# Two modulation units ahead of the tokens, and the opening's four up blocks taken in turns on six PSUM banks

## The chip, the cores and the metric

The kernel runs on one core of a Trainium2 chip as one program. The time is device microseconds from the first to the last instruction of a run. The five engines have a queue each: TensorE (PE; its weight loads are listed apart as PEld), VectorE (DVE), ScalarE (ACT), GpSimd (POOL) and SyncE (SP), which issues most of the DMA transfers.

## The reference

One layer of a diffusion backbone on 256 context tokens and 256 latent tokens of width 2048: a half-step SwiGLU feed-forward, a mixer (attention and mLSTM heads), a second feed-forward and a norm. The change lies in the first feed-forward's up product:

```python
def adaln(x, g, mod, i):
    return rms_norm(x, g) * (1 + mod[:, i + 1, None, :]) + mod[:, i, None, :]

def half_step_ffn(x, mod, i, g, w_up, w_down):
    h = adaln(x, g, mod, i)
    a, b = jnp.split(h @ w_up, 2, axis=-1)
    return x + 0.5 * mod[:, i + 2, None, :] * ((jax.nn.silu(a) * b) @ w_down)

# mod = (silu(c) @ w_mod + b_mod), one for the latent and one for the context tokens
```

Everything is fp32. The kernel gets that on TensorE by splitting each operand into a rounded part hi and a rest lo, and by three matmuls: hi x hi, lo x hi, hi x lo.

## The kernel before, in words

The hidden width 5632 is cut into 44 blocks of 128 (index f), each with a gate half a and a value half b. Before the first four blocks (f = 0 to 3) can be multiplied, shift and scale have to be made from the condition vector and `w_m0`, and the tokens have to be normalised. The kernel does all this at once in an **opening** that walks the 16 tiles of K (128 features each) in nine blocks: (0,1), (1,2), then seven of two tiles.

For each block of K:

- `mod_unit` loads pieces of the modulation weights (tile `mraw`, 1 MiB, four buffers), one unit each for the scale and the shift of a single K tile, four for a block of two. `mod_sums` multiplies a unit with the condition vector `cP` on TensorE; ScalarE copies the sums to `row`, TensorE turns them (`mod_turned`), and VectorE reduces them into the shift SH and the scale SC. One unit in four is multiplied on VectorE with `cB`, the condition vector spread over the partitions (`spread`, by matmuls with ones).
- `to_hT` (for the first two blocks `x_scaled`) transposes the normalised tokens `xs`, and `affine_split` makes hhi (ScalarE) and h and hlo (VectorE): the scaled and shifted tokens, split.
- `products` multiplies the block's rows of the up weights of f = 0, 1, 2 with them, into six PSUM banks `pre`. One transfer brings the block's weights (tile `raw`, three buffers); `split` makes hi (ScalarE, L118) and lo (VectorE, in the opening shown under L78). The products of a block are woven between the modulation sums of the next one.

Ahead of the blocks, the four token tiles (two of context, two of latent tokens, 1 MiB each) are loaded, squared on ScalarE (`sumsq`, L153), and scaled on VectorE (`x_tile`); their first columns are transposed (`x_turned`).

VectorE and TensorE are wrapped by `Pinned` in the opening: their instructions run in the order in which the code issues them, and the profile shows them all under L78, the wrapper's line. The SP queue is pinned as well. ScalarE's order is left to a scheduler, which works it out when the kernel is built.

After the opening `tail(f, pre[f])` takes silu(a) x b of f = 0, 1, 2 and stores it to `hidd[0]` (tile `ca`); f = 3 is done alone with 96 matmuls on whole weight tiles (`load_split`); then `quad(1)` begins, the first of the strip products that do four blocks f by seven products of half the size. It reads weight tiles `chain` and `raw`, whose splits VectorE makes, and sums of tokens (`token_forms`: n1, s2, s4, s3; tile `sraw`, and the lo parts n1l, s2l, s4l), which VectorE makes as well. A quad has 14 steps of 24 matmuls, each behind the split of one weight tile in two halves.

Of the kernel before, what the change touches and what calls it, by code (L numbers as in the profile page):

```python
# [19 lines left out]
P = 128  # L20
# [13 lines left out]
PACE2 = 70 / 73  # L34

BLOCKS = ((0, 1), (1, 2)) + tuple((k, k + 2) for k in range(2, 16, 2))
FB = 4
CB = 512
NCB = D // CB
# [10 lines left out]
def tile_layer(ctx: ExitStack, tc: tile.TileContext, I: dict, out: bass.AP):  # L50
# [13 lines left out]
    def bank():  # L64
        return ps["mm"].tile([P, 512], F32, tag="mm", name="mm")
# [265 lines left out]
    def pin(ins):  # L331
        tc.keep_in_program_order(ins)
# [111 lines left out]
    hlo = hpool.tile([P, KT, 512], F32R, tag="hl", name="hlo")  # L444

    pre = [[bank(), bank()] for _ in range(NPRE)]
    with pool(name="st", bufs=1) as st:
        scratch.append(st)
        cP = st.tile([P, KT, 32], F32, name="cP")
        nc.gpsimd.memset(cP, 0.0)  # L450
        pc = tbank()
# [52 lines left out]
        for s in (CTX, LAT):  # L504
            for t in range(2):
                x = xs0[s, t] = st.tile([P, D], F32, name=f"xs{s}{t}")
                tc.keep_in_program_order(nc.sync.dma_start(x, xsrc[s][t * P : (t + 1) * P, :]))
        tc.keep_in_program_order(nc.sync.dma_start(vecs, I["vecs"]))
        diagonals = [diagonal(s) for s in (CTX, LAT)]
        spread(CTX, diagonals[0])  # L510
        x_tile(CTX, 0)
        x_turned(0, CTX, 0)
        spread(LAT, diagonals[1])
        for s, t in ((CTX, 1), (LAT, 0), (LAT, 1)):
            x_tile(s, t, s == LAT and t == 1)
            x_turned(0, s, t)
# [5 lines left out]
        prods = iter(())  # L522
        unit = iter(range(32))

        def mod_unit():
            raw = st.tile([P, 2048], F32, tag="mraw", name="mraw", bufs=4)
            tc.keep_in_program_order(nc.sync.dma_start(raw, I["w_m0"][next(unit)]))
            return raw
# [33 lines left out]
                biased(i, k0, k1)  # L562
            turns.clear()

        turns = []
# [76 lines left out]
    with pool(name="f1u", bufs=1) as f1u:  # L642
# [7 lines left out]
        def ca_tile():  # L650
            return f1u.tile([P, CB], F32, tag="ca", name="ca", bufs=2)

        def tail(f, pab):
            sa = ca_tile()
            nc.scalar.activation(sa, pab[0], AF.Silu)
            nc.vector.tensor_tensor(sa, sa, pab[1], op=ALU.mult)
# [7 lines left out]

        for c in range(2):
            first_chain(1, c)
        for f in range(NPRE):
            tail(f, pre[f])
        for f in range(NPRE, FB):
            pab = []  # L670
            for ab in range(2):
                wt = load_split(I["w_up1"][f, ab])
                b = bank()
                for k in range(KT):
                    mm3(b, *wt(slice(k * P, (k + 1) * P)), hhi[:, k, :], hlo[:, k, :], k == 0, k == KT - 1)
                pab.append(b)
            tail(f, pab)


        n1, s2, s4 = form("n", "n1"), form("s", "s2"), form("t", "s4")  # L680
# [66 lines left out]
        def c12_tile():  # L747
            return f1u.tile([P, CB], F32, tag="c12", name="c12", bufs=2)

        def quad(n, after=lambda step: None):  # L750

# [1458 lines left out]
```

## Time and profile before

| | |
|---|---|
| time, median of 3 runs | 2666.89 us (2665.67 to 2669.02) |
| span of the profiled execution | 2666.8 us |
| TensorE busy | 2609.9 us (98%) |
| VectorE busy | 2130.1 us (80%) |
| ScalarE busy | 1347.2 us (51%) |
| granted TensorE clock, mean | 0.996 |
| DMA, mean | 255 GB/s |

In the rows of the timeline the first number is the start in us from the start of the span, the second the duration, then engine, line, operation, output tile <- input tiles, shape. Brackets give the idle time just before it and what released it. "SPq" is a DMA issue on SP's queue; in the list of DMA issues the last number is the median time in us from issue to landing. x4 means four such instructions joined in one row.

### The profile page before, as it was taken

Reading aid. Unit: us, or ns where it says so; the run is one execution under the profiler, and the core shown is the slowest. Engines: PE = TensorE matmul, PEld = TensorE weight load, DVE = VectorE, ACT = ScalarE, POOL = GpSimd, SP = SyncE. Lnnn points to the kernel's source line nnn. Section 1 sums busy time; section 2 is a strip of 40 time slices with the busy share of each in tenths; the row PEclk is TensorE's granted clock in tenths of the full one; section 3 lists DMA queues with packets and bytes.
Section 4 is the critical chain, followed back from the end, with each engine's and each line's share of the span. In section 5 each row is a group of like instructions: output and inputs, shape, how many; then the busy total and the mean of one; then the engine's idle time right before and its main releaser. Section 6 shows DMA issues by size and latency. Waiting matters only on the chain. (4 is left out here: it accounts for less than half of the span.)

```text
span 2666.8 us, 33730 instructions
## 1 busy us (share of the span) xinstructions
PE 2609.9 (98%) x12718; PEld 2158.4 (81%) x12718; DVE 2130.1 (80%) x2901; ACT 1347.2 (51%) x1682; POOL 221.6 (8%) x271
## 2 busy tenths in 40 slices
PE   8999999999999999999999999999999999999998
PEld 4688887888888878888889888877888888888886
DVE  5797878878888788888886979797688777777867
ACT  4354444544444565444454346355476655555554
POOL 0000001100000100000110000121000000000001
PEclk9999999999999999999999999999999999999999
DMA  9979999999999989889986866574579998989975
GB/s 346 351 213 270 263 279 260 258 276 281 264 280 273 266 230 239 229 209 234 225 233 224 309 229 225 205 260 166 172 249 284 295 286 292 289 277 281 277 230 168
DMA packets 135027, 679.97 MB, mean 255 GB/s; under 512 B 14152, under 2 KB 23624, under 8 KB 73552
## 3 DMA queue, kind: packets, MB, share of 16 engines
q1 hardware_dynamic: 107504, 500.59, 50.9%
q0 software_dynamic: 27360, 177.22, 34.0%
q8 instruction: 100, 1.64, 0.2%
q14 instruction: 63, 0.52, 0.1%
HBM read 659.87 MB, written 17.89 MB: 254 GB/s over the span
## 5 line engine op out<-in xcount | busy, mean ns | idle before, releaser
L118 ACT ACTIVATE hi<-raw 128x1024 fp32r<-128x1024 f32 (+3 forms) x542 | 560.7, 1038 | 639.0 <-PE mm L142 473.0
L119 DVE TENSOR_TENSOR lo<-raw,hi 128x1024 fp32r<-128x1024 f32 (+1 forms) x524 | 630.0, 1209 | 277.2 <-ACT hi L118 260.0
L118 ACT ACTIVATE hi<-chain 128x1024 fp32r<-128x1024 f32 x320 | 337.5, 1059 | 259.1 <-PE mm L142 129.1
L119 DVE TENSOR_TENSOR lo<-chain,hi 128x1024 fp32r<-128x1024 f32 x320 | 387.4, 1222 | 97.6 <-ACT hi L118 95.0
L140 PE MATMUL mm<-hi,hhi 128*128 128x512 f32 (+3 forms) x1024 | 392.5, 385 | 6.5 <-DVE c L744 6.0
L141 PE MATMUL mm<-lo,hhi 128*128 128x512 f32 (+3 forms) x1024 | 388.0, 379 | 1.7 <-DVE lo L119 1.5
L142 PE MATMUL mm<-hi,hlo 128*128 128x512 f32 (+3 forms) x1024 | 387.5, 379 | 0.0
L198 DVE SCALAR_TENSOR_TENSOR junk<-sraw,cBh 128x1024 fp8e5<-128x1024 f32 x192 | 234.4, 1221 | 23.2 <-DMA sraw<-in_w_mt 20.9
L140 PEld LDWEIGHTS mm<-hi,hhi 128*128 128x128 f32 x1024 | 192.8, 189 | 39.5 <-ACT hi L118 4.5
L141 PEld LDWEIGHTS mm<-lo,hhi 128*128 128x128 f32 x1024 | 193.1, 189 | 33.9 <-DVE lo L119 2.8
L142 PEld LDWEIGHTS mm<-hi,hlo 128*128 128x128 f32 x1024 | 192.8, 188 | 33.8
L142 PE MATMUL mm<-hi,hid2l 128*128 128x512 f32 x352 | 137.3, 390 | 0.0
L140 PE MATMUL mm<-hi,hid2h 128*128 128x512 f32 x352 | 137.2, 390 | 0.0
L141 PE MATMUL mm<-lo,hid2h 128*128 128x512 f32 x352 | 137.1, 390 | 0.0
L140 PE MATMUL mm<-hi,h2hi 128*128 128x512 f32 x320 | 125.0, 391 | 1.5 <-DVE sab L1802 1.5
L141 PE MATMUL mm<-lo,h2hi 128*128 128x512 f32 x320 | 124.6, 390 | 0.0
L142 PE MATMUL mm<-hi,h2lo 128*128 128x512 f32 x320 | 124.6, 389 | 0.0
L641 POOL DMA_DIRECT2D chain<-in_w_up1b x60 | 53.0, 883 | 742.3 <-DVE lo L119 606.9
L142 PE MATMUL mm<-hhi,lo 128*128 128x512 f32 (+1 forms) x288 | 100.4, 349 | 4.5 <-DVE lo L119 4.4
L140 PE MATMUL mm<-hhi,hi 128*128 128x512 f32 (+1 forms) x288 | 101.2, 351 | 0.0
L141 PE MATMUL mm<-hlo,hi 128*128 128x512 f32 (+1 forms) x288 | 99.5, 345 | 0.0
L198 DVE SCALAR_TENSOR_TENSOR sr<-sr,cBl 128x1024 f32<-128x1024 f32 x72 | 87.2, 1218 | 7.6 <-DMA sr<-in_w_mt 7.3
(474 smaller groups left out, 5499.3 us busy)
## 6 DMA issues: line engine op xcount, KB each, us to landing
raw<-in_w_dn SPq DMA_DIRECT2D x70, 1024.0 KB, 7.4
sraw<-in_w_mt SPq DMA_DIRECT2D x128, 512.0 KB, 7.5
chain<-in_w_up1b POOLq DMA_DIRECT2D x60, 1024.0 KB, 10.7
raw<-in_w_up2b SPq DMA_DIRECT2D x50, 1024.0 KB, 7.0
raw<-in_w_up1b SPq DMA_DIRECT2D x40, 1024.0 KB, 8.5
sr<-in_w_mt SPq DMA_DIRECT2D x69, 512.0 KB, 5.3
mraw<-in_w_m SPq DMA_DIRECT2D x32, 1024.0 KB, 7.2
chain<-in_w_dn POOLq DMA_DIRECT2D x30, 1024.0 KB, 8.7
```

The lines of the kernel that those rows point to most:

```text
L118: nc.scalar.activation(hi, src, AF.Copy)
L119: vector[0].tensor_tensor(lo, src, hi.bitcast(F32), op=ALU.subtract)
L140: tensor[0].matmul(out_ap, sh, mh, start=first, stop=False, skip_group_check=skip)
L141: tensor[0].matmul(out_ap, sh, ml, start=False, stop=False, skip_group_check=skip)
L142: tensor[0].matmul(out_ap, sl, mh, start=False, stop=last, skip_group_check=skip)
L198: ins = nc.vector.scalar_tensor_tensor(junk() if junk else raw, raw, 1.0, cB[s], op0=ALU.mult, op1=ALU.mult, accum_out=mT[:, i, s, kt, h : ...
L641: accum = lambda dst, src: nc.gpsimd.dma_start(dst, src, accum_op=ALU.add)
```

## The change

Four things change, all in the opening and the hand-over to quad 1.

1. The first two modulation units and the vectors `vecs` are issued ahead of the token tiles, and the modulation sums of block (0,1), its shift and scale and the split of its up weights are issued in the code before the token tiles' work, which is now in `tokens()`.
2. `products` is replaced by `columns`, which follows a plan. All four blocks f take part, three at a time on the six banks: f = 0, 1, 2 for K tiles 0 to 3; 1, 2, 3 for 4 to 9; 2, 3, 0 for 10 to 15. What a block f missed is made up: K 0 to 3 of f = 3 beside block 6, K 4 to 9 of f = 0 beside block 12 (`LATER`, generator `back`), and K 10 to 15 of f = 1 as a last group.
3. When f = 0 has its first 4 tiles and f = 1 its first 10, ScalarE copies both halves' partial sums to SBUF (tile `by`, one buffer) and SP stores them in DRAM (`put_by`); their banks go to another f. After the opening `firsts` loads them again, and `tail` adds them on VectorE to the rest of the sum, for f = 0 and f = 1 at steps 0 and 6 of quad 1.
4. A block's up weights come by one transfer for each f (three of 128x2x256 in place of one of 128x6x256).

The same 384 products of 128x512 are computed in both kernels.

The first place is VectorE from the start of the program: `raw<-cc,ident` prepares the spread, `cB` is its copy, `s` and `xs` are the token tiles' squares and scaling. Before:

```order
L78 TENSOR_TENSOR raw<-cc,ident 32x2048 x2
L78 COPY cB<-mm 128x512 x4
L78 TENSOR_REDUCE s_149<-ss_140 128x1
L78 TENSOR_SCALAR xs_119<-xs_119,rstd 128x256
L78 TENSOR_SCALAR xs_119<-xs_119,rstd 128x1792
...
L78 TENSOR_SCALAR xs_125<-xs_125,rstd 128x1792
L78 TENSOR_REDUCE SH<-tr 128x2
L78 TENSOR_TENSOR SH<-SH,vecs 128x2
L78 TENSOR_TENSOR lo<-raw,hi 128x384 x2
L78 TENSOR_REDUCE SC<-tr 128x2
```

and in the change:

```order
L94 TENSOR_TENSOR raw<-cc,ident 32x2048 x2
L94 TENSOR_TENSOR lo<-raw,hi 128x384 x2
L94 TENSOR_REDUCE SH<-tr 128x2
L94 TENSOR_TENSOR SH<-SH,vecs 128x2
L94 TENSOR_REDUCE SC<-tr 128x2
L94 TENSOR_TENSOR SC<-SC,vecs 128x2
L94 SCALAR_TENSOR_TENSOR SC<-SC,vecs 128x1 x2
L94 COPY cB<-mm 128x512 x4
L94 TENSOR_REDUCE s_217<-ss_208 128x1
L94 TENSOR_SCALAR xs_128<-xs_128,rstd 128x256
```

The weights' split and the making of shift and scale moved from behind the four token tiles to ahead of the cB copies and of the tiles. On ScalarE, at the same place, the split's other half has stayed behind the squares; in the change:

```order
L598 ACTIVATE row<-tr 128x128 x2
L169 ACTIVATE junk,ss_208<-xs_128 128x512 x4
L169 ACTIVATE junk,ss_233<-xs_130 128x512 x4
L169 ACTIVATE junk,ss_250<-xs_132 128x512 x4
L169 ACTIVATE junk,ss_267<-xs_134 128x512 x2
L134 ACTIVATE hi<-raw 128x384 x4
```

Here the copies of the two sums (`row`) come first now, and hi comes behind all 14 squares.

The third place is SP's queue at block (4,6), where the first partial sums are stored. Before, loads alone:

```order
L412 DMA raw<-in_w_up 128x6x256
L527 DMA mraw<-in_w_m 128x2048 x4
L412 DMA raw<-in_w_up 128x6x256
L527 DMA mraw<-in_w_m 128x2048 x4
L412 DMA raw<-in_w_up 128x6x256
```

and in the change, with the two stores and the weights of f = 3 for K 0 to 3 (128x2x512):

```order
L477 DMA raw<-in_w_up 128x2x256 x3
L578 DMA mraw<-in_w_m 128x2048
L506 DMA by_109<-by 128x512
L506 DMA by_110<-by 128x512
L477 DMA raw<-in_w_up 128x2x512
L578 DMA mraw<-in_w_m 128x2048 x3
L477 DMA raw<-in_w_up 128x2x256 x3
```

Three of the four units that followed the weights now stand behind both stores. At block (10,12) the queue has the same form with weights of 128x2x768.

The diff, cut to its core:

```diff
+COLUMN_PLAN = _column_plan()
+PUT_BY = {(0, 4): 3, (1, 10): 0}
+LATER = {6: (3, 0, 4), 12: (0, 4, 10)}
...
+        def columns(groups, early=False):
...
+                for f, k0, k1 in g:
+                    w = 2 * (k1 - k0) * P
+                    pin(nc.sync.dma_start(raw[:, o : o + w].rearrange("p (a c) -> p a c", a=2), I["w_up1"][f, :, :, k0 * P : k1 * P].rearrange("a p c -> p a c")))
...
+                    if (f, k1) in PUT_BY:
+                        for ab in range(2):
+                            t = st.tile([P, CB], F32, tag="by", name="by", bufs=1)
+                            nc.scalar.activation(t, slot[f][ab], AF.Copy)
+                            nc.sync.dma_start(put_by[f][ab], t)
+                            begun.discard((f, ab))
+                        del slot[f]
+                        slot[PUT_BY[f, k1]] = [bank(), bank()]
...
+        turns, back = [], iter(())
+        loaded.extend([mod_unit() for _ in range(2)])
+        pin(nc.sync.dma_start(vecs, I["vecs"]))
+        for s in (CTX, LAT):
+            for t in range(2):
+                x = xs0[s, t] = st.tile([P, D], F32, name=f"xs{s}{t}")
+                pin(nc.sync.dma_start(x, xsrc[s][t * P : (t + 1) * P, :]))
...
-        for k0, k1 in BLOCKS:
+        for (k0, k1), groups in zip(BLOCKS, COLUMN_PLAN):
             kk = slice(k0, k1)
-            following = products(I["w_up1"], pre, k0, k1, hhi, hlo, k0 == 0)
+            following = columns(groups, k0 == 0)
+            if k0 in LATER:
+                back = columns([[LATER[k0]]])
+                steps(back)
...
                     steps(prods, 3 - (k1 - k0))
-                if k0 == 0:
-                    mod_turned()
+                    steps(back)
...
             for s in (CTX, LAT):
                 scale_of(0, s, kk)
+            if not k0:
+                tokens()
...
-        def tail(f, pab):
-            sa = ca_tile()
-            nc.scalar.activation(sa, pab[0], AF.Silu)
-            nc.vector.tensor_tensor(sa, sa, pab[1], op=ALU.mult)
+        def tail(f, first=None):
+            a, b = slot[f]
+            if first:
+                for x, y in zip(first, (a, b)):
+                    nc.vector.tensor_tensor(x, y, x, op=ALU.add)
+                a, b = first
+            sa = a if first else ca_tile()
+            nc.scalar.activation(sa, a, AF.Silu)
+            nc.vector.tensor_tensor(sa, sa, b, op=ALU.mult)
...
-        for f in range(NPRE):
-            tail(f, pre[f])
-        for f in range(NPRE, FB):
...
+        first_of = {f: firsts(f) for f in (0, 1)}
+        tail(2)
+        tail(3)
...
         def first_steps(step):
+            if step in (0, 6):
+                tail(step // 6, first_of[step // 6])
```

More of the change, by code (lines that the diff above doesn't have):

```diff
@@ L36, with _column_plan @@
 BLOCKS = ((0, 1), (1, 2)) + tuple((k, k + 2) for k in range(2, 16, 2))
+def _column_plan():
+    out = []
+    for k0, k1 in BLOCKS:
+        fs = (0, 1, 2) if k1 <= 4 else (1, 2, 3) if k1 <= 10 else (2, 3, 0)
+        groups = [[(f, k0, k1) for f in fs]]
+        if k1 == KT:
+            groups.append([(1, 10, 16)])
+        out.append(groups)
+    return out
+COLUMN_PLAN = _column_plan()
+PUT_BY = {(0, 4): 3, (1, 10): 0}
+LATER = {6: (3, 0, 4), 12: (0, 4, 10)}
 FB = 4
@@ L446, in tile_layer, with load @@
     pre = [[bank(), bank()] for _ in range(NPRE)]
+    slot = dict(enumerate(pre))
+    put_by = {f: [dr.tile([P, CB], F32, name=f"by{f}{ab}") for ab in range(2)] for f in (0, 1)}
     with pool(name="st", bufs=1) as st:
         scratch.append(st)
+        begun = set()
+        def columns(groups, early=False):
+            def load(g):
+                n = sum(2 * (k1 - k0) * P for _, k0, k1 in g)
+                raw = raw_tile(n)
+                o = 0
+                for f, k0, k1 in g:
+                    w = 2 * (k1 - k0) * P
+                    pin(nc.sync.dma_start(raw[:, o : o + w].rearrange("p (a c) -> p a c", a=2), I["w_up1"][f, :, :, k0 * P : k1 * P].rearrange("a p c -> p a c")))
+                    o += w
+                return raw, n
+            ahead = load(groups[0])
+            if early:
+                wt = split(*ahead)
+            yield
+            for i, g in enumerate(groups):
+                if i or not early:
+                    wt = split(*ahead)
+                if i + 1 < len(groups):
+                    ahead = load(groups[i + 1])
+                o = 0
+                for f, k0, k1 in g:
+                    if f not in slot:
+                        slot[f] = [tbank(), tbank()]
+                    for ab in range(2):
+                        for k in range(k0, k1):
+                            new = (f, ab) not in begun
+                            begun.add((f, ab))
+                            mm3(slot[f][ab], *wt(slice(o, o + P)), hhi[:, k, :], hlo[:, k, :], new, k == KT - 1 or (f, k + 1) in PUT_BY)
+                            o += P
+                            if k % 2 or k1 - k0 == 1:
+                                yield
+                    if (f, k1) in PUT_BY:
+                        for ab in range(2):
+                            t = st.tile([P, CB], F32, tag="by", name="by", bufs=1)
[4 more added lines that the diff above has]
+                        slot[PUT_BY[f, k1]] = [bank(), bank()]
         cP = st.tile([P, KT, 32], F32, name="cP")
@@ L502, in x_turned @@
             tensor[0].transpose(tb[:, o : o + P], xs0[s, t][:, k * P : (k + 1) * P], ident)
[L504 to L516, printed above, removed]
         def x_scaled(k, tb):
@@ L523, in tile_layer @@
         unit = iter(range(32))
+        loaded = []
         def mod_unit():
+            if loaded:
+                return loaded.pop(0)
             raw = st.tile([P, 2048], F32, tag="mraw", name="mraw", bufs=4)
@@ L666, in tile_layer, with c12_tile @@
             first_chain(1, c)
-        for f in range(NPRE):
-            tail(f, pre[f])
-        for f in range(NPRE, FB):
[L670 to L677, printed above, removed]
+        def c12_tile():
+            return f1u.tile([P, CB], F32, tag="c12", name="c12", bufs=2)
+        first_of = {f: firsts(f) for f in (0, 1)}
+        tail(2)
+        tail(3)
         n1, s2, s4 = form("n", "n1"), form("s", "s2"), form("t", "s4")
```

17 lines of the change are left out of this document (14 added, 3 removed).

## The prediction

> **What bounds the kernel now.** I read the page first, then a table of short windows over the opening, then the timeline of its first 35 us, of one steady block and of the hand-over to the strip product.
>
> ```profile
> span 2666.8 us, 33730 instructions
> PE 2609.9 (98%) x12718; PEld 2158.4 (81%) x12718; DVE 2130.1 (80%) x2901; ACT 1347.2 (51%) x1682; POOL 221.6 (8%) x271
> ```
>
> The profiled execution took 2666.8 us against a median of 2666.89, so the sum below is made against 2666.8. TensorE is idle for 57 us in all. The change touches the opening and the first strip product only, so what matters is TensorE's state there (columns: window, its length, busy time of PE, PEld, DVE, ACT and POOL, granted clock, DMA share, GB/s).
>
> ```profile
> 0.00:10.00 10.00, 4.58 (x6) 2.00 (x7) 5.72 (x5) 5.27 (x13) 1.48 (x9) 1.00 0.77 300
> 10.00:20.00 10.00, 7.85 (x11) 2.80 (x10) 5.12 (x12) 7.63 (x20) 2.23 (x6) 1.00 1.01 402
> 20.00:30.00 10.00, 8.60 (x81) 4.39 (x83) 5.21 (x13) 2.57 (x6) 0.74 (x2) 1.00 0.85 324
> 60.00:70.00 10.00, 9.73 (x77) 7.26 (x80) 5.72 (x16) 4.40 (x10) 0.00 (x0) 1.00 1.02 410
> 130.00:140.00 10.00, 8.79 (x43) 6.88 (x42) 6.79 (x14) 5.56 (x9) 0.00 (x0) 1.00 0.25 89
> 140.00:150.00 10.00, 10.00 (x45) 8.27 (x45) 9.99 (x11) 3.77 (x5) 0.00 (x0) 1.00 1.03 386
> ```
>
> From 60 us on TensorE has about 0.27 us of idle time in ten; after 140 it has none. DMA moves 410 GB/s when it is full, which is 2.56 us for 1 MiB (1.049 MB). A block of two K tiles loads four modulation units of 1 MiB and 0.75 MiB of up weights, 4.75 x 2.56 = 12.2 us. In the next rows the same piece of two blocks, the first modulation sum, stands 66.68 - 51.71 = 15.0 us apart, so TensorE sets the pace and DMA has little to spare. From 66.68 on I use 13.7 us a block, the part without the waits that are seen at 53.81 and 54.68 (15.0 less 0.58, 0.37 and 0.33). One matmul of 512 columns takes 55.50 - 55.26, about 0.23 us.
>
> ```profile
> 51.71 1.08 PE L78 MATMUL tr<-mraw,cP 128*32 128x128 f32 x32 [0.33 <-DVE h L78]
> 53.81 0.50 PE L78 MATMUL mm<-hlo,hi 128*128 128x512 f32 x1 [0.58 <-DVE hlo L78]
> 54.68 0.50 PE L78 MATMUL mm<-hhi,lo 128*128 128x512 f32 x1 [0.37 <-DVE lo L78]
> 55.26 0.40 PE L78 MATMUL mm<-hlo,hi 128*128 128x512 f32 x1
> 55.50 0.40 PE L78 MATMUL mm<-hhi,lo 128*128 128x512 f32 x1
> 66.68 1.08 PE L78 MATMUL tr<-mraw,cP 128*32 128x128 f32 x32
> ```
>
> **The start: modulation weights ahead of the tokens.** Now the chain that leads to the first up product.
>
> ```profile
> 6.17 0.63 ACT L153 ACTIVATE junk<-xs 128x512 bf16<-128x512 f32 x1 [3.36 <-DMA xs<-in_ctx]
> 7.80 0.69 DVE L78 COPY cB<-mm 128x512 f32<-128x512 f32 x1
> 13.53 0.15 DVE L78 TENSOR_REDUCE s<-ss 128x1 f32<-128x4 f32 x1
> 15.44 7.19 PE L78 MATMUL mm<-raw,ones 32*128 32x512 f32 x8
> 15.96 0.63 ACT L153 ACTIVATE junk<-xs 128x512 bf16<-128x512 f32 x1
> 21.45 0.52 ACT L118 ACTIVATE hi<-raw 128x384 fp32r<-128x384 f32 x1
> 23.86 0.47 PE L78 MATMUL mm<-ident,xs 128*128 128x128 f32 x1 [0.61 <-DVE xs L78]
> 27.39 1.03 DVE L78 TENSOR_TENSOR lo<-raw,hi 128x384 fp32r<-128x384 f32 x2
> 29.74 1.94 PE L78 MATMUL tr<-mraw,cP 128*32 128x128 f32 x32
> 29.85 0.17 DVE L78 TENSOR_REDUCE SC<-tr 128x2 f32<-128x8 f32 x1 [1.43 <-PE tr L78]
> 30.44 0.56 ACT L379 ACTIVATE hhi<-mm,SH,SC 128x256 fp32r<-128x256 f32 x1 [1.16 <-DVE SC L78]
> 31.97 0.79 PE L78 MATMUL mm<-hhi,hi 128*128 128x512 f32 x1 [0.29 <-ACT hhi L379]
> ```
>
> Before, the first token tile lands at 6.17; ScalarE squares from then to 15.96 + 0.63 (14 pieces, one every 0.753 us); VectorE scales the four tiles from 13.53 until the last transpose at 23.86, 10.3 us; the sums of the first block follow on TensorE and the first product starts at 31.97. In the changed order two units and the vectors go first: the first token tile lands 2 x 2.56 + 0.4 = 5.5 us later, at 11.7. TensorE uses the gap for two sums that cost about 5 us on the path before.
>
> But VectorE is pinned to program order, and there the split of the first up weights, lo<-raw,hi, now stands ahead of the four cB copies and of all four token tiles. It needs ScalarE's hi, which stands behind the 14 squares. So: 11.7 + 9.8 + 0.6 = 22.1 for the last square; two hi pieces of 0.52 to 23.1; the second lo to 23.7; six small SH and SC operations, about 1.0 (0.6 of it is seen from 29.85 to 30.44), to 24.7; four copies of 0.69 to 27.5; the token tiles' 10.3 us to 37.8. The transpose and hhi come 0.6 later and the product 1.5 after hhi (30.44 to 31.97): 39.9. The third unit's sum on TensorE, 1.9 behind the last transpose, gives 40.2. The first product moves from 31.97 to about 40.1: **+8**. Behind it every block starts as many us later, since 13.7 us a block is TensorE's own time. Lower end +5, if tiles and squares overlap better than in the rows; upper end +10, if each tile waits its 2.56 us too.
>
> [...]
>
> **Matmuls moved.** Sixty of the fourth block's 96 products run in the opening (24 beside block 6, 36 beside block 12), and those of the other blocks that are left follow it: 60 x 0.23 = 13.8 us more before the opening's end, 13.8 us less behind it. TensorE is full on both sides, so this is **0**; the idle 0.27 us in ten, 1.9 us from 60 to 130, is all that could be won. The extra traffic, four stores and four loads of 0.25 MiB, lies in blocks made longer by these matmuls.
>
> **The partial sums put by.** Each pair is copied by ScalarE through one buffer and stored from SP's queue, and SP holds the loads of the next modulation units behind them.
>
> ```profile
> 48.97 0.43 SPq L412 DMA_DIRECT2D raw<-in_w_up  x1
> 49.49 10.90 SPq L527 DMA_DIRECT2D mraw<-in_w_m  x4
> 56.26 1.58 ACT L118 ACTIVATE hi<-raw 128x768 fp32r<-128x768 f32 x2 [3.12 <-DMA raw<-in_w_up]
> hid<-ca SPq DMA_DIRECT2D x4, 256.0 KB, 6.0
> cc<-in_cc SPq DMA_DIRECT2D x1, 16.0 KB, 1.7
> raw<-in_w_up SPq DMA_DIRECT2D x2, 384.0 KB, 12.5
> vecs<-in_vecs SPq DMA_DIRECT2D x1, 144.0 KB, 10.6
> ```
>
> Before, after the weights at 48.97, four units were issued in turn from 49.49 to 60.4, each as its buffer came free. In the changed order one unit, two stores and 0.5 MiB of weights come first, and then the three units of which the second is needed by the sum that was at 66.68, now 74.7. On the clock moved by 8: ScalarE's hi ends at 65.8 at the latest (56.26 + 1.58 + 8; 65.0 with the pieces landing one by one); the first copy ends 0.6 later and its store goes out at 65.7. It lands L later; only then the second copy of 0.6 may use the buffer, and its store is out at 66.5 + L. From there the queue carries 0.25 + 0.5 + 1 + 1 MiB, 7.0 us, after the 2.4 us that a lone 1 MiB takes beyond its 2.56 (4.9 in all, issued at 1.25 and landed at 6.17 above). The needed unit lands at 66.5 + L + 9.4 = 75.9 + L: TensorE stands still for 1.2 + L. The second pair has 0.75 MiB behind it and the copy stands behind only one hi, some 4.5 us into its block: 5.3 + L + 2.4 + 7.7 = 15.4 + L against 13.7, so 1.7 + L.
>
> L does not occur alone in the trace. From below, the 16 KB load took 1.7 and 0.25 MiB adds 0.6: 2.3. From above, the stores of hid took 6.0 in the median with loads ahead of them. The queue is nearly empty here, so I take 2.5: **+3.7 and +4.2**. The ends are +2 each (a copy that doesn't wait for hi gains 1.2) and about +7.5 each.
>
> [...]
>
> **The hand-over to the strip product.** Columns as in the timeline before.
>
> ```profile
> 136.41 1.82 DVE L78 TENSOR_TENSOR lo<-raw,hi 128x768 fp32r<-128x768 f32 x2
> 147.47 0.68 DVE L656 TENSOR_TENSOR ca<-ca,mm 128x512 f32<-128x512 f32 x1
> 149.20 1.22 DVE L703 TENSOR_TENSOR sraw<-sraw,hlo 128x1024 f32<-128x1024 f32 x1
> 150.41 1.23 DVE L688 TENSOR_TENSOR n1l<-sraw,n1h 128x1024 fp32r<-128x1024 f32 x1
> 188.91 1.23 DVE L119 TENSOR_TENSOR lo<-chain,hi 128x1024 fp32r<-128x1024 f32 x1 [0.52 <-ACT hi L118]
> 166.79 0.39 PE L142 MATMUL mm<-hhi,lo 128*128 128x512 f32 x1
> 167.01 0.39 PE L140 MATMUL mm<-hi,hhi 128*128 128x512 f32 x1
> ```
>
> VectorE works without a pause from 136.41 to 188.91, at 1.14 us for 1024 columns and 0.6 for 512, on splits and token sums that quad 1 needs from 167.01, 30.6 us after the last hlo. In the change quad 1 begins 13.8 us sooner, 16.8 after it. VectorE saves 4 x 1.14 (the fourth block's splits) and pays 2 x 0.9 for two more splits of 768 columns and 4 x 0.6 for the additions: about as much work in 13.8 us less. Adding up its order against 24 matmuls (5.4 us) a step, the splits keep ahead by 1.6 us or more through step 6; the two halves of step 7 are ready 55.4 and 57.7 us after the last hlo and wanted at 16.8 + 7 x 5.4 = 54.9 and at 56.2. So 1.5 us late, some 2.5 with ScalarE's hi ahead of each lo: **+2.5**. Ends: 0, if ScalarE and loads never hold VectorE, and +6, since 30.6 us of cover shrink to 16.8 and one late load of 4.9 would go through.
>
> **Sum:** 8 + 3.7 + 4.2 + 2.5 = 18.4; 2666.8 + 18.4 = **2685 us** (+0.7%). All low ends: 5 + 2 + 2 + 0 = 9, 2676; all high ends: 10 + 7.5 + 7.5 + 6 = 31, 2698.
>
> **Rivals.**
> - *Faster: the start is really won.* If the token tiles followed the squares alone, as before, the last transpose would be at 11.7 + 3.0 + 10.3 = 25.0 and the first product at 27.1, 4.9 us earlier; with the 1.9 us of idle time and the 1.2 us at 130 filled, 2659. For it: two sums run in time that TensorE did not use. Against it: even without lo in the way, the cB copies wait for the spread matmuls (one sequence takes 7.2 us at 15.44), which now stand behind two sums that end about 11; that alone puts the tiles at 19 and the product near 32, no gain. Chance 0.06.
> - *No change.* ScalarE or VectorE gets through the tiles in the shade and the stores land before the next unit matters: start 0 to 2, stores and hand-over 0 to 2, 2666 to 2671. For it: units wait in four buffers. Against it: three of the four units ahead are used up by 74.7. Chance 0.12.
> - *Larger loss at the stores and the hand-over.* L of 6 and VectorE 6 us late: 8 + 7.2 + 7.7 + 6 = 29, 2696 and up, from the point where the stores queue behind a full MiB each. Chance 0.08.
> - *DMA becomes the bound.* Each block's weights come in three pieces instead of one. If two pieces more each cost the lone 2.4 us, a block would take 12.2 + 4.8 = 17.0 against 13.7: +3.3 in seven blocks, 23 us beside the start's 8, 2698. Against it: from 10 to 20 us the queue held transfers of 144 and 384 KB and still moved 402 GB/s. Chance 0.04. [...]
>
> **How the numbers follow.** My forecast has 0.70. What a measurement of this kernel can tell from no change is about 0.2%, 5.3 us: under 2661.5 is faster, over 2672.2 slower. Faster 0.07 (the first rival and a little more), the same 0.12, slower 0.81. The range, 2665 to 2697, leaves out the first rival, the lower edge of the second and the tails above.
>
> **What would show it.** In the changed profile: the first mm<-hhi,hi near 40 us, with its wait on hhi behind token tiles, and lo<-raw,hi on VectorE ahead of them near 23; TensorE waiting 3 to 5 us on mraw at two first sums, near 75 and 125, with the second by store issued 2.5 us after the first; a wait on VectorE's lo near 40 us into quad 1; no idle time that is new elsewhere. A first product before 33 us, or units that land ahead of their sums, would make the forecast wrong.

## The result, and the profile after

| | before | after |
|---|---|---|
| time, median | 2667.95 us (4 runs, 2665.67 to 2675.87) | 2690.39 us (4 runs, 2688.36 to 2691.54) |
| span of the profiled execution | 2666.8 us | 2688.7 us |
| TensorE busy | 2609.9 us | 2616.8 us |

The change makes the kernel slower: the ratio of the times is 1.0083, with a 95% interval of 1.0069 to 1.0098. The spans are 21.9 us apart, and that is the number that the traces have to explain. TensorE is busy for 7 us more with the same 12718 matmuls and transposes, so part of the loss is time in which it works more slowly.

The page's first lines, after:

```profile
span 2688.7 us, 33790 instructions
PE 2616.8 (97%) x12718; PEld 2163.0 (80%) x12718; DVE 2129.7 (79%) x2907; ACT 1353.5 (50%) x1688; POOL 221.7 (8%) x271
```

The table of windows, after (columns as before: PE, PEld, DVE, ACT, POOL, granted clock, DMA share, GB/s):

```profile
10.00:20.00 10.00, 8.61 (x22) 3.02 (x14) 0.00 (x0) 8.53 (x24) 0.00 (x0) 1.00 1.02 412
20.00:30.00 10.00, 1.96 (x3) 1.01 (x4) 5.67 (x16) 3.64 (x10) 1.46 (x4) 1.00 1.03 419
70.00:80.00 10.00, 6.43 (x55) 5.09 (x54) 7.43 (x9) 4.17 (x9) 0.00 (x0) 0.80 0.97 376
80.00:90.00 10.00, 10.00 (x60) 6.75 (x59) 2.65 (x5) 1.23 (x2) 0.00 (x0) 0.85 1.03 428
120.00:130.00 10.00, 6.08 (x33) 4.73 (x31) 6.20 (x14) 4.32 (x8) 0.00 (x0) 1.00 0.97 350
130.00:140.00 10.00, 9.34 (x72) 6.84 (x72) 5.23 (x6) 0.28 (x1) 0.00 (x0) 0.83 1.03 418
```

Three places stand out. From 20 to 30 us TensorE is busy for 2 us of 10, where it was busy for 8.6. In the windows at 70 and 120 it stands still for about 4 us. And in the windows at 70, 80 and 130, with the first wait and behind both, the granted clock is 0.80 to 0.85, where every row of the opening had 1.00 before.

**The start.** The timeline after, up to the first product:

```profile
11.40 0.63 ACT L169 ACTIVATE junk<-xs 128x512 bf16<-128x512 f32 x1 [0.44 <-DMA xs<-in_ctx]
22.39 1.03 DVE L94 TENSOR_TENSOR lo<-raw,hi 128x384 fp32r<-128x384 f32 x2 [14.65 <-ACT hi L134]
24.14 2.48 DVE L94 COPY cB<-mm 128x512 f32<-128x512 f32 x4
26.53 0.15 DVE L94 TENSOR_REDUCE s<-ss 128x1 f32<-128x4 f32 x1
36.80 0.48 PE L94 MATMUL mm<-ident,xs 128*128 128x128 f32 x1 [0.54 <-DVE xs L94]
37.20 1.93 PE L94 MATMUL tr<-mraw,cP 128*32 128x128 f32 x32
39.06 0.80 PE L94 MATMUL mm<-hhi,hi 128*128 128x512 f32 x1
```

VectorE stands for 14.65 us at the split of the first up weights, until ScalarE's hi behind the squares; then come the copies and the four tiles. The first product is at 39.06, against 31.97: **+7.1**.

**The partial sums put by.** The queue of SP, the second of ScalarE's two copies, the list of DMA issues, TensorE around block 6 and at block 12, and two windows (columns as above):

```profile
56.61 0.43 SPq L578 DMA_DIRECT2D mraw<-in_w_m  x1
64.47 3.03 SPq L506 DMA_DIRECT2D by<-by  x2
68.37 1.41 SPq L578 DMA_DIRECT2D mraw<-in_w_m  x3
...
66.55 0.60 ACT L505 ACTIVATE by<-mm 128x512 f32<-128x512 f32 x1 [2.11 <-DMA by<-by]
...
by<-by SPq DMA_DIRECT2D x4, 256.0 KB, 2.2
...
73.65 0.39 PE L94 MATMUL mm<-hhi,lo 128*128 128x512 f32 x1
77.61 1.93 PE L94 MATMUL tr<-mraw,cP 128*32 128x128 f32 x32 [3.57 <-DMA mraw<-in_w_m]
79.47 0.80 PE L94 MATMUL mm<-hhi,hi 128*128 128x512 f32 x1
80.06 0.63 PE L94 MATMUL mm<-hlo,hi 128*128 128x512 f32 x1
80.49 0.63 PE L94 MATMUL mm<-hhi,lo 128*128 128x512 f32 x1
84.01 1.07 PE L94 MATMUL tr<-mraw,cP 128*32 128x256 f32 x16
...
130.66 1.94 PE L94 MATMUL tr<-mraw,cP 128*32 128x128 f32 x32 [4.59 <-DVE lo L94]
136.23 1.07 PE L94 MATMUL tr<-mraw,cP 128*32 128x256 f32 x16
...
76.10:82.90 6.80, 5.29 (x40) 4.27 (x41) 6.55 (x8) 0.28 (x1) 0.00 (x0) 0.50 1.04 416
130.70:134.10 3.40, 3.40 (x36) 2.73 (x37) 3.37 (x3) 0.28 (x1) 0.00 (x0) 0.50 1.05 397
```

SP issues nothing from 57.0 to 64.5 and three units at 68.4, as foreseen. TensorE waits 3.6 and 4.6 us. (The second wait is put down to VectorE's lo, but the unit of that sum landed at 130.5.) What follows is new: the sum takes 1.93 where it took 1.08 before, and the first products behind it start every 0.43 us in place of 0.23. In the two windows the granted clock is 0.50: from 76.1, 2 us into the first wait, to 82.9, and from the end of the second wait, 130.7, to 134.1. From the sum to the next one it is 84.01 - 77.61 = 6.4 us and 136.23 - 130.66 = 5.6, while an undisturbed stretch of that kind (one sum, 12 products) takes 4.0 (run e6 below). So **3.6 + 2.4** at the first and **4.6 + 1.6** at the second; the longer wait has the shorter slow stretch. Sixty matmuls have moved across the opening's end, and at the start of quad 1 the lag, by which everything is later than before, is 18.4 us: 0.9 less than these parts add up to.

**The hand-over.** Quad 1 after, which begins at 185.4:

```profile
224.90 0.50 PE L157 MATMUL mm<-lo,s4h 128*128 128x512 f32 x1 [0.38 <-DVE lo L135]
229.41 4.89 SPq L243 DMA_DIRECT2D sraw<-in_w_mt  x2
239.88 1.22 DVE L214 SCALAR_TENSOR_TENSOR junk<-sraw,cBh 128x1024 fp8e5<-128x1024 f32 x1 [2.31 <-DMA sraw<-in_w_mt]
241.03 0.68 DVE L823 TENSOR_TENSOR c<-mm,c 128x512 f32<-128x512 f32 x1
241.86 0.47 PE L156 MATMUL mm<-hi,hhi 128*128 128x512 f32 x1 [1.26 <-DVE c L823]
```

The late lo of step 7 costs 0.7 us (the lag goes from 18.4 to 19.0). The larger part comes later: VectorE stands at a sum over later modulation weights (`sraw`), whose load has not landed; behind it, in fixed order, is the addition c that frees TensorE's bank. A second wait, 1.4 us for ca at 269.0, has a longer chain: VectorE waited 3.1 us for ScalarE's hi there, and ScalarE 3.0 us for weights (`chain`) that SP had issued between the loads of sraw. The load of sraw is late because its buffer is: SP issues it at 229.4, when VectorE has done its last token sum in that buffer, 44 us into quad 1; before, that was 25 us into it. After quad 1 the lag is 21.9, so **+3.5** here; in this run it is about the same at the end (22.1).

### The profile page after: what moved, and what is told of

It is laid out like the page before. It is cut to its first block, busy times and chain, and to the rows that moved or that the text cites. A ratio compares the mean times of both kernels' runs of the same rounds, so it can differ in the third digit from the quotient of the medians.

```text
span 2688.7 us, 33790 instructions
## 1 busy us (share of the span) xinstructions
PE 2616.8 (97%) x12718; PEld 2163.0 (80%) x12718; DVE 2129.7 (79%) x2907; ACT 1353.5 (50%) x1688; POOL 221.7 (8%) x271
## 5 line engine op out<-in xcount | busy, mean ns | idle before, releaser
L134 ACT ACTIVATE hi<-raw 128x1024 fp32r<-128x1024 f32 (+4 forms) x544 | 562.5, 1037 | 634.3 <-PE mm L158 473.9
L135 DVE TENSOR_TENSOR lo<-raw,hi 128x1024 fp32r<-128x1024 f32 (+2 forms) x520 | 625.5, 1210 | 268.5 <-ACT hi L134 252.0
L158 PE MATMUL mm<-hhi,lo 128*128 128x512 f32 (+1 forms) x256 | 87.9, 343 | 4.5 <-DVE lo L135 4.4
L156 PE MATMUL mm<-hhi,hi 128*128 128x512 f32 (+1 forms) x256 | 88.8, 347 | 0.0
L157 PE MATMUL mm<-hlo,hi 128*128 128x512 f32 (+1 forms) x256 | 87.0, 340 | 0.0
```

Source lines behind the costliest of these rows:

```text
L134: nc.scalar.activation(hi, src, AF.Copy)
L135: vector[0].tensor_tensor(lo, src, hi.bitcast(F32), op=ALU.subtract)
L156: tensor[0].matmul(out_ap, sh, mh, start=first, stop=False, skip_group_check=skip)
L157: tensor[0].matmul(out_ap, sh, ml, start=False, stop=False, skip_group_check=skip)
L158: tensor[0].matmul(out_ap, sl, mh, start=False, stop=last, skip_group_check=skip)
```

## The experiments

"Lag" is how much later than in the kernel before the same matmul starts in a run's trace: first at the start of quad 1, then after quad 1, then at the last matmul of the program. Each is read from one profiled execution. Behind quad 1, where only e10 and e12 are edited, the lag still moves by up to 4 us either way, so differences of that size in the last column are not given to an edit. Differences in the text are taken before rounding.

| run | edit | ratio to before (95%) | lag, start of quad 1 | lag after it | lag at the end |
|---|---|---|---|---|---|
| the change | | 1.0083 (1.0069 to 1.0098) | 18.4 | 21.9 | 22.1 |
| e1 | start alone, on the kernel before | 1.0033 (1.0020 to 1.0046) | 6.6 | 6.4 | 7.3 |
| e2 | change with the old start | 1.0065 (1.0046 to 1.0084) | 11.4 | 15.7 | 13.2 |
| e4 | split behind the tiles | 1.0077 (1.0062 to 1.0092) | 18.1 | 21.9 | 19.6 |
| e5 | stores on ScalarE's queue | 1.0098 (1.0081 to 1.0115) | 20.6 | 24.2 | 25.7 |
| e6 | filler matmuls | 1.0071 (1.0059 to 1.0083) | 14.5 | 23.5 | 19.1 |
| e7 | no additions | 1.0066 (1.0051 to 1.0081) | 16.0 | 20.0 | 17.6 |
| e8 | ScalarE's queue, two buffers | 1.0051 (1.0039 to 1.0064) | 6.5 | 15.3 | 11.4 |
| e9 | start mended, on the kernel before | 0.9989 (0.9981 to 0.9998) | -1.2 | -1.4 | 0.2 |
| e10 | e8, later sums later | 1.0048 (1.0034 to 1.0062) | 6.7 | 7.8 | 7.1 |
| e11 | start mended again, on the kernel before | 0.9984 (0.9975 to 0.9992) | -2.9 | -3.1 | -6.0 |
| e12 | plan with all mended | 0.9999 (0.9990 to 1.0007) | -3.6 | -2.5 | -1.9 |
| e13 | two buffers, SP's queue | 1.0084 (1.0070 to 1.0098) | 17.1 | 20.8 | 18.3 |

**e1: the start alone.** The kernel before, with the loads and the emission order of the change's start.

```diff
+        loaded.extend([mod_unit() for _ in range(2)])
+        pin(nc.sync.dma_start(vecs, I["vecs"]))
...
             for s in (CTX, LAT):
                 scale_of(0, s, kk)
+            if not k0:
+                tokens()
```

> The kernel before with the start alone changed: two units and the vectors ahead of the tokens, and the first block's sums, its shift and scale and the split of its weights ahead of the token tiles; three up blocks at a time as before, nothing put by. Theory: the start is a loss that is carried to the end, since every later block is TensorE's own time: first product near 39 us, as in the change (39.06 against 31.97), and 2667 + 7 = 2674 to 2675. Rival: the blocks behind have slack, and the loss shows only together with the stores: within 2 us of before.

Median 2677.09 against 2667.81. The first product is at 39.08, as in the change, and the lag is the same at the end of the opening. So the start alone is a loss, and nothing behind it gives the time back. By medians it is 9 us, a little more than the 7 of the trace; the interval, 5 to 12 us, holds both.

**e2: everything but the start.**

```diff
-        loaded.extend([mod_unit() for _ in range(2)])
-        pin(nc.sync.dma_start(vecs, I["vecs"]))
...
+        pin(nc.sync.dma_start(vecs, I["vecs"]))
+        tokens()
         for (k0, k1), groups in zip(BLOCKS, COLUMN_PLAN):
```

> The change with the start of the kernel before: tokens first, vectors, then the units; the plan of columns, the partial sums put by and the hand-over stay. Theory of separate terms: 22 us of loss less the start's 7, so 2667 + 15 = 2682, with TensorE waiting 3 to 5 us twice before a first modulation sum. Rival: the stores hurt only because the start has eaten the lead of the loads; then the waits at the two sums shrink below 1 us and it comes to within 5 us of before.

Median 2684.97 (its four runs lie between 2681 and 2692), lag 11.4 where the change has 18.4: at that place the 7 us of the start, and nothing else, are gone. The waits are there as in the change, 3.8 and 4.7 us and a short one, in the list of TensorE's waits (engine, line, what for; us in all, times, longest):

```profile
PE tr L94 <- DMA mraw<-in_w_m: 8.8, 3, 4.7
```

The rival falls: the stores hurt with the old start too.

**e4: the split behind the tiles.**

```diff
             ahead = load(groups[0])
             if early:
+                yield
                 wt = split(*ahead)
...
                 tokens()
+                steps(following)
```

> The change with one thing moved: the split of the first up weights (lo on VectorE) is issued behind the four token tiles in place of ahead of them; shift and scale of the first block stay ahead. Theory: the split, which waits for ScalarE's squares until 22.4, is what holds the tiles; without it they wait for the cB copies (spread ends at 18.6) and the first product comes 4 to 7 us sooner, at 32 to 35 us, and the time falls by as much, to 2683 to 2686. Rival: the tiles are held by their landing or by the spread of the latent condition: no gain over 1 us.

The first product comes at 38.22, only 0.8 us sooner, and the time (2689.03) can't be told from the change's. The theory falls, and the rival holds: the spread of the latent condition. The timeline shows what took the split's place:

```profile
23.36 0.60 ACT L538 ACTIVATE cB<-mm 128x512 f32<-128x512 f32 x1 [5.88 <-PE mm L94]
23.85 0.62 ACT L169 ACTIVATE junk<-xs 128x512 bf16<-128x512 f32 x1
28.48 0.60 ACT L538 ACTIVATE cB<-mm 128x512 f32<-128x512 f32 x1 [1.11 <-PE mm L94]
30.47 0.16 DVE L94 TENSOR_REDUCE s<-ss 128x1 f32<-128x4 f32 x1 [6.19 <-ACT junk L169]
```

ScalarE's order, which the scheduler made anew, now has the copies of the latent spread among the squares of the third tile. They wait for TensorE's spread until 28.5, and the tile waits with the squares. The split was the wait that ended last, but with it gone another of nearly the same length holds the tiles.

**e5 and e13: stores on another queue, or a second buffer.** One line each; e13 also has two in place of three buffers for `row`, as there was no room otherwise.

```diff
-                            nc.sync.dma_start(put_by[f][ab], t)
+                            nc.scalar.dma_start(put_by[f][ab], t)
```

```diff
-                            t = st.tile([P, CB], F32, tag="by", name="by", bufs=1)
+                            t = st.tile([P, CB], F32, tag="by", name="by", bufs=2)
```

> The change with the four stores of the partial sums issued from ScalarE's queue in place of SP's; still one buffer. Theory: the units come late because SP stands at the two stores while their buffers are free; without them the waits of 3.6 and 4.6 us vanish, and the slow matmuls behind them (about 2.3 and 1.5 us) with them: 12 us less than the change, about 2678. Rival: DMA itself is full there, and the units land as late as before: no change. Rival: the waits go and the slow matmuls stay: 8 us less.

> The change with two buffers for the partial sums put by (and two for the sums' rows), the stores still on SP's queue. Theory: what makes the units late is that SP, in its order, stands at the stores until the second product of the pair is done and copied (the first store went out at 64.5, while the unit behind it could have been issued at 60); the wait of 2.2 us for the first store's landing hides behind that product, so a second buffer brings 0.5 us at each pair: 2688 to 2690, with waits of 3 and 4 us left. Rival: the single buffer is the cause, the waits go: 2679 to 2681, as with both mended.

e5 is not faster: its median, 2695.27, is 4.9 us above the change's (the intervals overlap), and its lag at quad 1 is 2.2 us larger. ScalarE's and TensorE's timelines:

```profile
64.40 0.34 ACTq L506 DMA_DIRECT2D by<-by  x1
72.99 0.60 ACT L505 ACTIVATE by<-mm 128x512 f32<-128x512 f32 x1 [8.62 <-DMA by<-by]
73.92 0.69 PE L94 MATMUL tr<-ident,row 128*128 128x128 f32 x2 [5.49 <-ACT row L598]
```

SP is free now and its loads run ahead; the store, issued beside them, takes 7.9 us in the median in place of 2.2. The second copy waits for it with ScalarE's whole queue behind it, among it the row that TensorE has to turn. The wait has moved from SP to ScalarE. No rival of mine had that.

e13 (2689.74) leaves SP standing at the stores: it issues the first at 64.04 and the second by 66.5, and the three units from 67.8, 0.6 us sooner than in the change. TensorE waits 4.0 and 4.5 us, where the change has 3.6 and 4.6. So neither edit alone helps, and the rival, by which the waits go, falls. The median is 0.65 us below the change's; a gain of 0.5 us from the buffer, as expected, can't be told from none.

**e8: both.**

> The change with the stores of the partial sums on ScalarE's queue and two buffers for them (and two in place of three for the sums' rows, to make room). Now neither SP's loads nor ScalarE's later work waits for a store. Theory: the two waits of 3.6 and 4.6 us and the slow matmuls behind them (3.8) go: 10 to 12 us less than the change, 2678 to 2680; what stays is the start's 7 and the hand-over's 3.6. Rival: the loads are late whatever the stores do, since the weights made up beside the two blocks (0.5 and 0.75 MiB) come at the same time: half of it stays, 2684.

The opening is mended: SP's units are issued as their buffers come free, and the two long waits on mraw are gone (what is left is one of 3.0 us for the very first unit, as in the change, and one of 0.4). The row of SP's queue, then TensorE's largest wait from 180 to 260 us, and the window from 258.3 on:

```profile
60.20 6.26 SPq L578 DMA_DIRECT2D mraw<-in_w_m  x3
...
PE tr L818 <- DVE ca L824: 4.1, 1, 4.1
258.30:265.10 6.80, 5.27 (x15) 4.34 (x16) 6.54 (x10) 3.28 (x5) 0.88 (x1) 0.50 0.79 201
```

The lag at quad 1 is 6.5, which is the start alone (6.6 in e1): the plan and its stores cost nothing in the opening any more. Twelve us are won there, and 8.7 of them reach the median (2681.70). At the hand-over the lag grows by 8.7 in place of 3.5: 0.7 at the late lo, 1.5 at a wait for c, and 6.6 where TensorE waits 4.1 us for ca, with the granted clock at 0.50 until 265.1. Part of that comes back behind quad 1 (lag 11.4 at the end), in places that no run here takes apart.

**e6: filler.** Sixteen matmuls right before the two sums that wait.

```diff
+            if k0 in (7, 13) and not i:
+                for _ in range(16):
+                    tensor[0].matmul(w, hhi[:, 0, :P], hhi[:, 0, :], start=True, stop=True)
```

> The change with 16 matmuls of 128x512 more on TensorE right ahead of the first modulation sum of block 6 and of block 12 (into a bank that the sum overwrites), some 3.7 us of work each, so that TensorE works in most of the time in which it stood still there (3.6 and 4.6 us). They need nothing that is late. Theory: the sum can't start before its unit lands, so the work costs nothing, and TensorE doesn't fall to the slow rate (matmuls 0.43 in place of 0.23 us) behind the wait, which was 2.3 us at the first and 1.5 us at the second: 3 to 4 us less than the change, about 2687, with more work done. Rival: the slow matmuls have another cause (the loads landing beside them): then no change, or up to 1 us more.

```profile
73.61 3.79 PE L94 MATMUL tr<-hhi 128*128 128x512 f32 x16
77.40 1.08 PE L94 MATMUL tr<-mraw,cP 128*32 128x128 f32 x32
78.99 0.39 PE L94 MATMUL mm<-hhi,lo 128*128 128x512 f32 x1
79.22 0.40 PE L94 MATMUL mm<-hhi,hi 128*128 128x512 f32 x1
81.36 1.07 PE L94 MATMUL tr<-mraw,cP 128*32 128x256 f32 x16
```

The sum starts when it did (77.40 against 77.61), but it takes 1.08 us, the products start every 0.23 and the next sum comes at 81.36 in place of 84.01. At quad 1 the lag is 14.5, 3.8 us less than in the change, with 7.3 us of work more, and the granted clock is 1.00 in the windows from 70 to 90 and from 120 to 140. The loads land beside the sum as they did, so the rival falls: the slow stretch is caused by TensorE's standing still, and was worth 2.4 + 1.6 = 4.0 us as read above. The hand-over then loses 9.0 us in this run, again with a wait for ca (3.9 us) and 6.8 us at a granted clock of 0.50, so that after quad 1 nothing of the gain is left (23.5 against 21.9). The median is 3 us below the change's all the same (2687.41, the intervals overlap); the trace has these 3 us too (19.1 against 22.1 at the end), but they come back behind quad 1, so the time alone does not show what the filler is worth.

**e7: no additions.** The four additions of the partial sums are left out, and with them this part of the result.

```diff
-                for x, y in zip(first, (a, b)):
-                    nc.vector.tensor_tensor(x, y, x, op=ALU.add)
-                a, b = first
```

> The change without the four additions of 128x512 on VectorE by which the partial sums put by are added to the rest for f = 0 and 1 (loads, silu, product and stores stay); this part of the result is left out. Theory: the hand-over's 3.6 us are VectorE's backlog, so 2.4 us of work less takes 2 to 3 us of it: 2687.5. Rival: what is lost there is the cover itself, 13.8 us of matmuls that now lie ahead, and the additions are hidden: under 1 us.

Median 2686.25. The lag at step 7 no longer grows: the late lo of 0.7 us goes with the additions. The wait for c stays, and is 1.9 us long; behind it TensorE runs at a granted clock of 0.50 for 3.4 us, and 3.9 us are lost in quad 1 all the same. Without that slow stretch (1.7 us) it would be 2.2 in place of 3.5, so the additions are about 1.3 of the hand-over, and the rest has another cause. Of the 4.1 us between the medians, 2.3 lie ahead of quad 1 in the traces, where nothing was edited.

**e10: the later sums later.** On e8: VectorE's first sums over `sraw` three steps later (`lead` is 3 there and 0 for all other callers). Only the first two loads stay where they are; each later one is issued when a sum lets its buffer go, so it comes later too (the third at 234.7 in place of 222.1).

```diff
-        waits = 0
+        waits = lead
```

> The run with ScalarE's queue and two buffers, and the first of the later modulation sums (junk<-sraw on VectorE, from step 8 of quad 1 on) issued three steps, 16 us, later; their loads stay where they are. There VectorE stood 5.2 us on the load of sraw and TensorE 5.1 us behind it (c and ca), 6.6 to 6.8 us of the lag arose at that place. Theory: the hand-over's loss is this late load, which VectorE takes in fixed order ahead of what TensorE needs; with the sums later it goes, and 6 us with it: 2675 to 2676. Rival: VectorE has too much work for 13.8 us of cover less, whatever it waits for: at most 1 to 2 us are won, and TensorE waits on lo or c elsewhere in quad 1.

VectorE's waits from 200 to 260 us in e8, and TensorE's from 180 to 260 in e10:

```profile
DVE junk L214 <- DMA sraw<-in_w_mt: 5.2, 2, 3.2
```

```profile
PE tr L818 <- DVE ca L824: 0.5, 1, 0.5
PE mm L157 <- DVE lo L135: 0.4, 1, 0.4
```

In quad 1 the lag now grows by 1.1 in place of 8.7, so the later sums with their loads, and the slow stretch behind the wait, were the hand-over's loss there. As the edit moves most of the loads as well, it does not separate VectorE's standing at them from the room that they take on SP's queue ahead of the weights; and it was tried on e8, not on the change itself. But the median falls by 2.9 only (2678.78), and the two intervals overlap: a wait of 2.9 us for c, which e8 does not have, stands at about 300 us. The place of the loss in quad 1 is shown; what the delay is worth in all is not.

**e9, e11, e12: mending the start.** e9 is the kernel before with the units ahead of the tokens, but TensorE does the context spread first, VectorE takes copies, tiles and split in that order, and ScalarE's squares and first rows are in fixed order. It comes out between theory and rival: the first product is 2.6 us sooner, the median 2665.25 against 2668.35, with an interval that only just leaves out no change. e11 loads the two context tiles first and the units between them and the latent tiles, and scales the context tiles between the copies (its edit, cut to the loads):

```diff
             for t in range(2):
                 x = xs0[s, t] = st.tile([P, D], F32, name=f"xs{s}{t}")
                 pin(nc.sync.dma_start(x, xsrc[s][t * P : (t + 1) * P, :]))
+            if s == CTX:
+                units = [mod_unit() for _ in range(2)]
+                pin(nc.sync.dma_start(vecs, I["vecs"]))
...
```

e12 is the change's plan with e11's start, e8's stores and e10's delay.

> The kernel before (three up blocks at a time, nothing put by) with two units and the vectors ahead of the tokens, but the work at the start put in another order: the spread of the context condition first on TensorE, then the two sums; on VectorE the copies of the spread, then the token tiles, then the split; on ScalarE the squares and the first two rows in a fixed order, then the split and the copies of the latent spread. Theory: the first product comes at 27 to 28 us, 4 us sooner than before, and is carried to the end: 2663 to 2664, faster than both. Rival: something else holds the tiles (their landing, 5.4 us later than before; the spread of the latent condition): first product at 31 or later and no change.

> The kernel before with the start ordered once more: the two context tiles first, then the two units and the vectors, then the two latent tiles; the context tiles are scaled between the copies of the spread. Theory: in the run before it (first product at 29.4) ScalarE's squares, which began at 11.4 and ended at 23.8, held the last tile; with the context tiles ahead they begin at 6 and end near 21, the first product comes at 26, 6 us sooner than in the kernel before, and the time is 2662 to 2663. Rival: the last tile's landing or the spread holds it: first product at 28 or later, the gain stays near 3 us.

> The change's plan of columns with everything mended: that second start, stores on ScalarE's queue with two buffers, later sums three steps later. Theory: the plan of columns is neutral by itself, since TensorE has the same 384 products and no idle time to fill: within 2 us of the second start alone, 2662 to 2665. Rival: the hand-over, with 13.8 us of cover less, loses 2 us or more for good: 2666 to 2670. Rival: the plan gains once its faults are gone, 2 us or more below the second start alone.

The first products of e9, e11 and e12, and e11's longest wait for a unit:

```profile
29.39 0.80 PE L78 MATMUL mm<-hhi,hi 128*128 128x512 f32 x1
```

```profile
26.38 0.80 PE L78 MATMUL mm<-hhi,hi 128*128 128x512 f32 x1
PE tr L78 <- DMA mraw<-in_w_m: 2.4, 1, 2.4
```

```profile
26.34 0.80 PE L94 MATMUL mm<-hhi,hi 128*128 128x512 f32 x1
```

e11 is faster than both kernels: 2662.89 against 2668.31, ratio 0.9984 (0.9975 to 0.9992), 4 us with an interval of 2 to 7. Its first product is 5.6 us sooner; a unit that lands late then holds TensorE for 2.4 us, and the granted clock is 0.50 for 3.4 us from 54.6, so 2.9 are left at quad 1. e12 with the plan of columns is back at the time of the kernel before (2667.28), 4.4 us above e11 in the same comparison, though at the start of quad 1 it is even 0.7 ahead of it. So the plan with its mends is not neutral, and the first theory falls: the time is that of the rival (2666 to 2670). After quad 1 the two are 0.6 us apart in their traces, at the end 4.0, so most of it arises later than the rival had it. Whether it comes from the cover taken from VectorE or from the delayed sums (e12 has a wait of 2.6 us for c at 300 us, as e10 has) stays open.

## Why the prediction was right, and where its terms were off

It said 2685 (2665 to 2697), slower with 0.81; the time is 2690.39. The two places of the loss in the opening and their mechanisms were right; one cost was left out, and that the hand-over came out near is luck. Four terms were named:

- **Start, +8: right, 7.1.** The chain went as worked out (22.4 for the split, 24.1 copies, 26.5 tiles, 36.8 last transpose, 39.06). e1 shows that it is carried. But the sentence that even without the split nothing is gained "with the product near 32" was wrong in its number: e4 gave 38.2, since ScalarE's order was made anew and set the copies of the latent spread among the squares. I had priced the rival with an order that I had not looked at.
- **Matmuls moved, 0: right in size.** The 0.9 us by which the lag at quad 1 is smaller than its parts would fit the 1.9 us of idle time; that is a remainder, and no run shows where it was won.
- **Stores, +3.7 and +4.2: the waits were right, the step short.** The store's L was 2.2 (taken: 2.5) and the waits 3.6 and 4.6. What the step missed is the 4.0 us of slow matmuls behind them: a wait was priced by its length alone. e6 shows the cause. Behind both waits the trace shows a granted clock of 0.50 and products every 0.43 us in place of 0.23. How long a wait brings that on is not settled by these runs: the clock fell 2 us into the first wait, 3.4 us at 0.50 also came with a wait of 2.4 us (e11) and one of 1.9 (e7), and none with waits of 1.3 (e6), 2.1 (e12) and 2.5 us (e2). The slow matmuls are a term that the sum lacked.
- **Hand-over, +2.5: the size near, 3.5, by luck; the wait that was forecast is a fifth of it.** The late lo of step 7 came where it was foreseen, 39.5 us into quad 1, and cost 0.7. The other 2.8 are the waits for c and ca, behind the late loads of sraw and of the weights between them. VectorE's lost cover is behind these too, but I counted only its work, and not the loads that its buffers let go later. How much this place can cost is seen in e6 and e8, with 9.0 and 8.7, some 2.5 of it slow matmuls behind a wait of 3.9 or 4.1 us. That it costs more the faster the opening is, is not shown: e2, with a faster opening than e6, lost 4.3.

The sum, 18.4, falls 3.5 short of the 21.9 between the spans: 4.0 too little for the slow matmuls, 1.0 for the hand-over, and 0.3 at the waits, less 0.9 each at the start and for the idle time.

Of the signs that were named, the last did not hold: the waits for c and ca in quad 1 are idle time that is new elsewhere. The rivals: the faster one fell (first product at 39.1). The split into three transfers cost nothing that shows: with three pieces a block, the window at 80 us moved 428 GB/s. The larger loss named the right two places, but with a store of 6 us; in the change it was 2.2, and only from ScalarE's queue was it longer (7.9 in e5, 8.2 in e8).

## What to carry to other kernels

A piece put ahead on a queue of fixed order takes with it all that it waits for (here VectorE stood 14.65 us at the split put ahead, until ScalarE's hi, with the copies and the four tiles behind it): when a load goes first, see which engine's next instruction needs something that is now later, and look at the order of each engine again after every edit, the scheduled ones too. The waits of TensorE of 3.6 and 4.6 us cost 2.4 and 1.6 us beyond their length here, in slow matmuls; count both, and look at the granted clock behind shorter waits too (0.50 behind one of 1.9 us in e7). A stall that is mended ahead of another late load may be worth only what that load leaves (e8 won 12 us in the opening and then lost 8.7 at the hand-over, in place of 3.5), so follow the lag to the next place where it can be lost before giving a gain to an edit.

## What the runs showed of the hardware

- Filling a wait with work brought what follows forward: 16 matmuls more (3.8 us) before a sum took 2.6 us off the start of the next one, as TensorE kept its rate of a product every 0.23 us in place of 0.43.
- Behind the waits read here the granted clock was 0.50 for 3.4 or 6.8 us, and the longer wait did not have the longer stretch: 6.8 us with the wait of 3.6, of which TensorE worked in 5.3, and 3.4 with the wait of 4.6.
- The same store of 256 KB landed in 2.2 us from SP's queue, where at most the end of one earlier load was still landing, and in 7.9 and 8.2 us (e5, e8) from ScalarE's queue while SP's loads ran: another issuing engine did not pass them.
